# Experts' slot tables by a product with one-hot slots on chip, and three smaller moves, in a hybrid encoder block

## The chip, the core and the metric

One core of a Trainium2 chip runs the whole program. The metric is the device time of one execution in microseconds (us). Before the change three runs took 1166.63, 1168.26 and 1171.79 us; their median, 1168.26, is the time that the change is held against. The engines are TensorE (PE, with its weight loads as PEld), VectorE (DVE), ScalarE (ACT), GpSimd (POOL) and SyncE (SP), which here issues most of the DMAs.

## The reference, cut to what matters

`x` is 1024 tokens of 1024 float32. A mixing part (gated linear attention and indexer-selected attention, merged by gates) gives `mixed`. Then come the output projection, a norm and a two-level mixture of 32 experts, of which each token takes two:

```python
x = x + mixed @ w_out
h = rms_norm(x, g_ffn)
g_logits = h @ w_rg + b_rg                     # 4 groups
g_sel, g_w = argmax(g_logits), softmax(g_logits)[g_sel]
top_v, top_i = top_k((h @ w_re + b_re)[group g_sel], 2)   # of 8 experts in the group
top_w = softmax(top_v) * g_w
for e in range(32):
    hid = silu(h @ w_gate[e]) * (h @ w_up[e])  # D_EXPERT = 128
    y += combine[:, e] * (hid @ w_down[e])
x = x + y
```

## The kernel before, in words

Everything up to the output projection is untouched. Tokens lie in eight tiles of 128. The order of work on each engine is set by a planner that goes by the order of the program and its own cost estimates; a few orders are written out by hand with `add_manual_dep` (SCHED: order of issue only; SYNC: a real wait).

**Projection stage** (lines 821 to 922). `project(i, hf)` multiplies tile i by half `hf` of `w_out` (512 columns): 24 products, three for each of eight blocks of rows, since both factors are split into a high and a low float32r part. `norm_half` adds `x` (line 848, VectorE, into `x1`), transposes the half tile (851), copies it out (852, ScalarE), multiplies it by the 36 router columns (854) and sums squares (857). `norm_route` does the second half, writes `x1` to `out` (866, GpSimd's queue), takes the root by a chain of small VectorE operations (870 to 876), forms the logits (877) and, in `rows`, multiplies the whole row by the root and the gain (881, VectorE) and writes it to `h2d` in DRAM (886, GpSimd's queue).

**Routing.** `Moe.route(i0, i1)` does tiles 0-1, 2-3, 4-5 in pairs between the projections, then tile 6 and tile 7 each by itself. First-of-maximum (1002 to 1006) is five VectorE operations, used for the group and for each of two experts. The choice of a tile is `cn` (128 tokens x 32 experts, 0 or 1). Its rank in the expert comes from two small products per tile (1028 with a triangle of ones, 1031 with the counts so far). From the rank, the slot number is formed (1048 to 1054), and an indirect DMA per tile and pick (1056, GpSimd) scatters the pair (token, weight) to a table `tab` in DRAM with a row for each slot and expert; at the start it was filled with out-of-range tokens. An expert has 96 slots (R = 96) in the main pass.

**Between routing and experts**, `finish_routing` loads the first 96 rows of the table to SBUF (1067, ScalarE's queue), and counts the blocks of 96 beyond the first that each expert needs (1080 to 1095). That list goes to DRAM and back as one row (1097, 1099).

**Experts** (`Moe.run`). For each of 32 experts: gather 96 rows of `h2d` by the table's tokens (1142, GpSimd, indirect), transpose them (1151) and split them (1153, 1154), split the weights (1127 on ScalarE, 1128 on VectorE), multiply by gate and up (1135), form the hidden row (1162 to 1164), transpose it (1169), multiply by down (1177), scale by the token's weight (1180, 1182), and scatter with addition to `out` (1185, GpSimd, indirect). Gathers run five experts ahead in four buffers; `AC` is a ring of four buffers for results. Weights (1.5 MB an expert) are loaded on SP's queue (967, 970, 971) to eight buffers, the first eight experts' during the projection stage. From the ninth on, the gate half's load waits until the gather three experts ahead of the buffer's last user has landed (`late`), and the rest stands behind it or is put ahead by the planner. The first four gathers are issued together; buffers 3 and 4 are cleared before that (1111).

**End.** Each engine reads the number of further blocks from the list (1225), and a loop (1226) runs over them; in these runs its body is not entered. Line 1266 is the code that closes the program.

The `[P, ...]` scratch `V(kb, n)` is a place in one large SBUF tile `G`, which is why so many rows below are named G.

Of the kernel before, what the change touches and what calls it, by code (L numbers as in the profile page):

```python
# [61 lines left out]
def _constants():  # L62
# [20 lines left out]
    oh = np.zeros((P, 512 + 2 * NE * NB), np.float32)  # L83
    oh[:, 384:512] = np.eye(P)[::-1]
    oh[:, 512:512 + NE * NB] = np.repeat(np.arange(NE), NB)[None, :]
    oh[:, 512 + NE * NB:] = np.tile(np.arange(NB) + 1, NE)[None, :]
# [8 lines left out]
def block_kernel(ctx, tc, x, g_mix, w_in, w_alpha2, b_alpha, g_gla, w_br_gla, g_q, g_k, rel_bias, w_br_att,  # L95
# [702 lines left out]
    x1t = [p5.tile([P, 1024], F32, name=f"x1{j}")[:, :] for j in range(3)]  # L798
    h2t = [V(53, 1024), p5.tile([P, 1024], F32, name="h2b")[:, :]]
# [29 lines left out]
    def project(i, hf):  # L829
        if hf == 0:  # L830
            pws[i] = bankA(f"pw{i}")
        mm3(pws[i][:, hf, :], KT, lambda k: mh[i % 2][:, k, :], lambda k: ml[i % 2][:, k, :],
            lambda k: woh[hf][:, k, :], lambda k: wol[hf][:, k, :])
# [6 lines left out]
    def norm_half(i, hf):  # L840

        x1, h2 = x1t[i % 3], h2t[i % 2]
        hT = hTt.rearrange("p (k t) -> p k t", k=KT)
        if hf == 0:
            parts[i] = bankC(f"plg{i}"), ring("ss2", 2, 2)
        plg, ss = parts[i]
        xh = x1[:, 512 * hf:512 * hf + 512]
        nc.vector.scalar_tensor_tensor(xh, pws[i][:, hf, :], 0.5, xh, op0=ALU.mult, op1=ALU.add)
        pt = bankB(f"ph{i}{hf}").rearrange("p (b t) -> p b t", b=4)
        for k in range(4):  # L850
            nc.tensor.transpose(pt[:, k, :], xh[:, k * P:(k + 1) * P], ident)
        nc.scalar.activation(hT[:, 4 * hf:4 * hf + 4, :], pt, AF.Copy)
        for k in range(4 * hf, 4 * hf + 4):
            q = nc.tensor.matmul(plg[:, :36], hT[:, k, :], wr[:, k, :], start=(k == 0), stop=(k == KT - 1))
            if i == NT - 1 and k == 4:
                after(q, moe.rank)
        nc.scalar.activation(h2[:, 512 * hf:512 * hf + 512], xh, AF.Square, accum_out=ss[:, hf:hf + 1])
        if hf == 0:
            nc.vector.tensor_scalar(ss[:, 0:1], ss[:, 0:1], 1.0 / D, EPS, op0=ALU.mult, op1=ALU.add)

    def norm_route(i):
        ts_ = slice(i * P, (i + 1) * P)
        x1, h2 = x1t[i % 3], h2t[i % 2]
        norm_half(i, 1)
        plg, ss = parts.pop(i)
        nc.gpsimd.dma_start(out[ts_, :], x1)
        dump(f"x1_{i}", x1)
        rs = ring("rs", 1, 2)
        v, t, r = (ring(f"{k}_1", 1, 2) for k in ("nv", "nt", "nr"))
        nc.vector.scalar_tensor_tensor(v, ss[:, 1:2], 1.0 / D, ss[:, 0:1], op0=ALU.mult, op1=ALU.add)  # L870
        nc.vector.tensor_scalar(r.bitcast(I32), v.bitcast(I32), 1, None, op0=ALU.logical_shift_right)
        nc.vector.tensor_scalar(r.bitcast(I32), r.bitcast(I32), -1.0, float(MAGIC), op0=ALU.mult, op1=ALU.add)
        nc.vector.tensor_scalar(v, v, -0.5, None, op0=ALU.mult)
        for k in range(3):
            nc.vector.scalar_tensor_tensor(t, r, v, r, op0=ALU.mult, op1=ALU.mult)
# [3 lines left out]
        def rows(late=None):  # L879

            q = nc.vector.scalar_tensor_tensor(*(t.rearrange(m, k=KT) for t, m in (
                (h2, "t (k p) -> t k p"), (x1, "t (p k) -> t k p"))), rs, gffn.rearrange("t (p k) -> t k p", k=KT),
                op0=ALU.mult, op1=ALU.mult)
            if late:
                after(q, late)
            nc.gpsimd.dma_start(h2d[ts_, :], h2)
        return rows
# [9 lines left out]
    for i in range(NT):  # L897
# [6 lines left out]
        if i:  # L904
            if i == NT - 1:
                project(i - 1, 1)
            norm_route(i - 1)()
        norm_half(i, 0)
# [6 lines left out]
        else:  # L915
            project(i, 1)
        if i and i % 2 == 0:
            moe.route(i - 2, i)
    moe.route(6, 7)
    rows = norm_route(7)  # L920
    rows(moe.route(7, 8))
# [6 lines left out]
    moe.finish_routing(dump)  # L928
    if stop == "disp":
        return  # L930
    moe.run(vp2, stop)


class Moe:


    def __init__(self, nc, tc, V, C, bankA, bankB, bankC, drp, h2d, out, lg, tab, onehot, w_gate, w_up, w_down, ident, raws):
# [8 lines left out]
        self.feb = V(57, 2 * NE * NB)  # L946
        nc.sync.dma_start(self.feb, onehot[:, 512:])
# [12 lines left out]
    def load(self, j, wg=None, wu=None, wd=None, late=None):  # L960
# [9 lines left out]
        nc.sync.dma_start(raw[0][:, 1024:2048], wu.rearrange("(p k) c -> p (k c)", p=P))  # L970
# [3 lines left out]
    def route(self, i0, i1, early=None):  # L974
# [25 lines left out]
        def first_max(dst, src, tie, w, m):  # L1000

            nc.vector.tensor_reduce(m, src, axis=AX.X, op=ALU.max)
            nc.vector.tensor_tensor(dst, src, bc(m[:, :, None], [P, n, w]), op=ALU.is_equal)
# [6 lines left out]
        tmp, eg = big(n, 4, 8), big(n, 8)  # L1010
        nc.vector.tensor_mul(tmp, el, bc(ohg[:, :, :, None], [P, n, 4, 8]))
        nc.vector.tensor_reduce(eg, tmp.rearrange("p i g e -> p i e g"), axis=AX.X, op=ALU.add)
# [4 lines left out]
        s1, s2 = big(n, 4, 8), big(n, 4, 8)  # L1017
        cn = tmp
        for s, oh in ((s1, oh1), (s2, oh2)):
            nc.vector.tensor_mul(s, bc(ohg[:, :, :, None], [P, n, 4, 8]), bc(oh[:, :, None, :], [P, n, 4, 8]))  # L1020
        nc.vector.tensor_add(cn, s1, s2)
        cnf = cn.rearrange("p i g e -> p i (g e)")
        for i in range(n):
            nc.vector.tensor_add(self.cum[:, i0 + i + 1, :], self.cum[:, i0 + i, :], cnf[:, i, :])
        pp = self.bankB(f"prank{i0}")
        for i in range(n):
            s = slice(i * NE, (i + 1) * NE)
            q = nc.tensor.matmul(pp[:, s], C("lt"), cnf[:, i, :], start=True, stop=False)
            if early:
                self.tc.add_manual_dep(q.ins, early.ins.name, SCHED, reason="order of issue")  # L1030
            self.rank = nc.tensor.matmul(pp[:, s], C("ones"), self.cum[:, i0 + i, :], start=False, stop=True)
# [6 lines left out]
        nc.vector.tensor_reduce(gs, ex, axis=AX.X, op=ALU.add)  # L1038
        nc.vector.scalar_tensor_tensor(gs, dd, 1.0, gs, op0=ALU.add, op1=ALU.mult)
        nc.vector.tensor_scalar(gs, gs, 2.0, None, op0=ALU.mult)  # L1040
        nc.vector.reciprocal(w12[:, 0, :], gs)
        nc.vector.tensor_mul(w12[:, 1, :], w12[:, 0, :], dd)
        pos, rowf = big(n, NE), big(2, n)
        row = big(2, n).bitcast(I32)
        val = big(2, n, 2)
        nc.vector.tensor_copy(val[:, :, :, 0].bitcast(I32), bc(C("tok")[:, None, i0:i1], [P, 2, n]))
        nc.vector.tensor_copy(val[:, :, :, 1], w12)
        nc.vector.scalar_tensor_tensor(pos, pp[:, :n * NE].rearrange("p (i e) -> p i e", i=n), float(NE),
                                       bc(C("iota_e")[:, None, :], [P, n, NE]), op0=ALU.mult, op1=ALU.add)
        for k, s in enumerate((s1, s2)):  # L1050
            s = s.rearrange("p i g e -> p i (g e)")
            nc.vector.tensor_mul(s, pos, s)
            nc.vector.tensor_reduce(rowf[:, k, :], s, axis=AX.X, op=ALU.add)
            last = nc.vector.tensor_copy(row[:, k, :], rowf[:, k, :])
            for i in range(n):
                s = nc.gpsimd.indirect_dma_start(
                    out=self.tab, out_offset=bass.IndirectOffsetOnAxis(ap=row[:, k, i:i + 1], axis=0),
                    in_=val[:, k, i, :].bitcast(I32), in_offset=None, bounds_check=SLOTS * NE - 1, oob_is_err=False)
# [3 lines left out]
        return last  # L1062

    def finish_routing(self, dump):
        nc, C, V, tab = self.nc, self.C, self.V, self.tab
        tabs = self.tabs = self.keep(NE * 2).rearrange("p (e w) -> p e w", e=NE)
        nc.scalar.dma_start(tabs[:R].rearrange("p e w -> p (e w)").bitcast(I32),
                          tab[0:R * NE, :].rearrange("(s e) w -> s (e w)", e=NE))
        dump("tabs", tabs[:R])

        o = [12 * 256]

        def big(m):
            o[0] += m
            assert o[0] <= 18.5 * 256
            return V(o[0] / 256 - m / 256, m)
# [18 lines left out]
        self.routed = nc.vector.tensor_copy(lsti[:, 3:4], tot)  # L1095
        lstd = self.drp.tile([P, 4], I32, name="lstd")
        nc.scalar.dma_start(lstd, lsti)
        self.lrow = V(26, 512, I32)
        nc.scalar.dma_start(self.lrow[0:1, :], lstd.rearrange("p w -> (p w)")[None, :])
# [14 lines left out]
    def run(self, vp, stop):  # L1114
        nc, tc, V, ident = self.nc, self.tc, self.V, self.ident
        self.begin(vp, 1)
        NR, XG = len(self.raws), self.XG
        AC = [V(o, 1024) for o in (68, 72, 53, 12)][:4]
        HD = [V(57 + 1.5 * j, 384) for j in range(2)]
# [77 lines left out]
        idx = lambda j: self.tabs[:R, self.order[j], 0:1].bitcast(I32)  # L1197
        wgt = lambda j: self.tabs[:R, self.order[j], 1:2]
# [9 lines left out]
        for j in range(NE):  # L1208
# [16 lines left out]
        ntot = nc.values_load(self.lrow[0:1, 3:4], min_val=0, max_val=24)  # L1225
# [45 lines left out]
```

## Time and profile before

| | |
|---|---|
| median of three runs | 1168.26 us |
| profiled execution | 1172.33 us, span 1170.5 us |
| TensorE busy | 1083.0 us (93% of the span) |
| VectorE busy | 886.5 us (76%) |
| ScalarE, GpSimd busy | 506.7 us, 306.4 us |
| mean granted TensorE clock | 0.968 |
| DMA | 140.16 MB, mean 120 GB/s |

The profile is one execution. Times in it are from the span's start. In a row of the timeline the bracket gives the idle time of the engine before the instruction and who ended it; in the chain, each row is one link of the work that ended last. Busy engines off that chain cost nothing.

### The profile page before, as it was taken

To read this page: it belongs to the slowest core of one execution; us is meant where nothing else is said; L and a number is where in the kernel's file an instruction comes from. 1 tells how busy PE (TensorE), PEld (TensorE's weight loads), DVE (VectorE), ACT (ScalarE), POOL (GpSimd) and SP (SyncE) were. 2 spreads that over 40 slices of the span, in tenths; PEclk is the share of its full clock that TensorE was granted. 3 is DMA by queue.
4 is the path that set the end of the run, shared out by engine and by line. 5 is a ranking of instruction groups with operands and counts; after the bars stand their busy time and mean duration, and the time that the engine had idled before them with its cause. 6 is when DMAs were issued, how large, how long until landed. Compare 5 with 4: busy or idle time off the path is not lost.

```text
span 1170.5 us, 18890 instructions
## 1 busy us (share of the span) xinstructions
PE 1083.0 (93%) x7068; PEld 921.2 (79%) x7068; DVE 886.5 (76%) x1747; ACT 506.7 (43%) x1126; POOL 306.4 (26%) x259
## 2 busy tenths in 40 slices
PE   6999998999999999999999999998999659989883
PEld 5998897988788889999867888887778547767662
DVE  5689999999999999994388795552656667866662
ACT  5565626231211125554578764111222226655551
POOL 0100025231131131121043200161022356654422
PEclk9999999999999999999999999998999869998987
DMA  7111111034223231110001006575442669999982
GB/s 255 37 37 37 39 37 39 25 103 145 72 96 121 72 106 58 38 37 18 1 19 38 29 28 227 168 255 168 152 136 91 216 193 292 274 253 287 295 257 40
DMA packets 73104, 140.16 MB, mean 120 GB/s; under 512 B 12282, under 2 KB 47283, under 8 KB 73012
## 3 DMA queue, kind: packets, MB, share of 16 engines
q1 hardware_dynamic: 62482, 112.67, 29.3%
q0 software_dynamic: 10272, 26.25, 8.5%
q8 instruction: 56, 0.92, 0.3%
q14 instruction: 36, 0.29, 0.1%
q10 hardware_dynamic: 258, 0.03, 0.0%
HBM read 115.54 MB, written 31.76 MB: 126 GB/s over the span
## 4 chain that ended last, share of the span: by engine, by line
PE 61%; DVE 17%; DMA 12%; issue 4%; ACT 3%; POOL 0%; SPq 0%; POOLq 0%; DVEq 0%; ACTq 0%
PE pg L236 15%; PE pqkv L236 8%; PE py L236 7%; PE pw L236 5%; DVE G L717 4%; PE pgu L1135 4%; DMA raw<-in_w_gate_dram 4%; PE pv L236 4%; DVE G L716 3%; PE pav L641 3%; DVE G L387 3%; PE pPT L628 3%; PE pidx L236 3%; DMA rawx<-in_w_up_dram 2%; DMA raw<-in_w_down_dram 2%
## 5 line engine op out<-in xcount | busy, mean ns | idle before, releaser
L716 DVE MAX8 G<-G 128x8 f32<-128x384 f32 (+5 forms) x192 | 171.0, 893 | 4.6
L717 DVE MATCH_REPLACE8 G<-G 128x384 f32<-128x384 f32 (+5 forms) x192 | 168.0, 875 | 0.0
L236 PE MATMUL pg<-Qa,Q 128*128 128x512 f32 x512 | 159.8, 392 | 0.0
L228 POOL TENSOR_TENSOR Q<-G,Q 128x2048 fp32r<-128x2048 f32 x13 | 60.8, 4676 | 214.9 <-ACT Q L227 214.9
L236 PEld LDWEIGHTS pg<-Qa,Q 128*128 128x128 f32 x512 | 96.0, 188 | 21.0 <-issue 0.9
L236 PE MATMUL pg<-Qb,Q 128*128 128x512 f32 x256 | 99.6, 389 | 0.0
L236 PE MATMUL pv<-Q,Qa 128*128 128x256 f32 x512 | 94.8, 285 | 0.0
L236 PE MATMUL pqkv<-Q,Qa 128*128 128x256 f32 x512 | 92.2, 283 | 0.0
L236 PEld LDWEIGHTS pv<-Q,Qa 128*128 128x128 f32 x512 | 80.1, 191 | 2.1 <-issue 1.5
L236 PEld LDWEIGHTS pqkv<-Q,Qa 128*128 128x128 f32 x512 | 79.9, 192 | 0.1
L1185 POOL DMA_INDIRECT out_dram<-G x32 | 55.8, 1745 | 65.5 <-ACT G L1180 21.7
L236 PE MATMUL pv<-Q,Qb 128*128 128x256 f32 x256 | 72.5, 283 | 0.0
L236 PE MATMUL pqkv<-Q,Qb 128*128 128x256 f32 x256 | 72.5, 283 | 0.0
L227 ACT ACTIVATE Q<-G 128x2048 fp32r<-128x2048 f32 x20 | 38.2, 1911 | 78.4 <-PE pg L236 77.0
L1135 PE MATMUL pgu<-Qb,xt0h 128*96 128x256 f32 x256 | 54.4, 311 | 6.9 <-ACT xt0h L1153 6.9
L596 POOL TENSOR_TENSOR sm<-Tb,G 128x256 f32<-128x256 f32 x48 | 35.3, 741 | 96.0 <-DVE G L614 62.6
L1142 POOL DMA_INDIRECT xg<-h2d,G x32 | 47.7, 1491 | 46.1 <-DVE xt0l L1154 20.6
L236 PEld LDWEIGHTS pg<-Qb,Q 128*128 128x128 f32 x256 | 48.1, 188 | 10.2 <-issue 0.5
L1128 DVE TENSOR_TENSOR Qb<-G,Qb 128x1024 fp32r<-128x1024 f32 x32 | 38.6, 1217 | 21.2 <-ACT Qb L1127 21.0
L1135 PEld LDWEIGHTS pgu<-Qb,xt0h 128*96 128x96 f32 x256 | 40.6, 182 | 17.5 <-ACT xt0h L1153 17.4
L619 ACT ACTIVATE sm<-sm,G 128x128 f32<-128x128 f32 (+7 forms) x64 | 49.3, 771 | 7.2 <-DVE G L614 6.6
L1135 PE MATMUL pgu<-Qb,xt1h 128*96 128x256 f32 x256 | 51.8, 303 | 0.0
(292 smaller groups left out, 2870.7 us busy)
## 6 DMA issues: line engine op xcount, KB each, us to landing
G<-in_w_in_dram SPq DMA_DIRECT2D x20, 1024.0 KB, 5.2
gd<-G SPq DMA_DIRECT2D x16, 512.0 KB, 2.6
G<-gd SPq DMA_DIRECT2D x16, 512.0 KB, 4.5
G<-in_w_down_dram SPq DMA_DIRECT2D x16, 512.0 KB, 16.7
G<-in_w_gate_dram SPq DMA_DIRECT2D x16, 512.0 KB, 13.5
G<-in_w_up_dram SPq DMA_DIRECT2D x16, 512.0 KB, 20.8
raw<-in_w_gate_dram SPq DMA_DIRECT2D x12, 512.0 KB, 10.3
raw<-in_w_up_dram SPq DMA_DIRECT2D x12, 512.0 KB, 18.4
```

The source lines that it names most:

```text
L227: nc.scalar.activation(hi, r3, AF.Copy)
L228: (eng or nc.vector).tensor_sub(lo, r3, f(hi))
L236: nc.tensor.matmul(o, a, b, start=(i == 0), stop=(i == len(seq) - 1))
L387: nc.vector.scalar_tensor_tensor(scv, rl, wisc[:, i, h:h + 1], scv, op0=ALU.mult, op1=ALU.add)
L596: nc.gpsimd.tensor_tensor(band, Tb[:, h, :], sc[i][:, n1:], op=ALU.add)
L619: nc.scalar.activation(sm[:, :W], sm[:, :W], AF.Exp, scale=-1.0, bias=nm[:, 1:2], accum_out=rs8s[i][:, h:h + 1])
L716: nc.vector.max(out=m8, in_=sc[i])
L717: nc.vector.match_replace(out=sc[i], in_to_replace=m8, in_values=sc[i], imm_value=SENT)
L1128: q = nc.vector.tensor_sub(lo[:, n], r, hi[:, n].bitcast(F32))
L1135: nc.tensor.matmul(o, a, b, start=(i == 0), stop=(i == len(seq) - 1))
L1142: gathered[j] = nc.gpsimd.indirect_dma_start(out=XG[j % 4][:R], out_offset=None, in_=self.h2d, in_offset=bass.IndirectOffsetOnAxis(ap=idx, ...
L1185: return nc.gpsimd.indirect_dma_start(out=self.out, out_offset=bass.IndirectOffsetOnAxis(ap=idx, axis=0), in_=AC[j % 4][:R], in_offset=Non ...
```

## The change

- **One-hot slots.** `route` becomes `choose`, `place` and `enter`. `choose` makes the picks as before (one operation less in a first-of-maximum of a single tile), and masks `s` (expert of pick k) and `ve` (the same times token - 1024, and times weight). `place` reduces each pick's rank to one number per token (`tensor_tensor_reduce`), compares it with 0..95 to a one-hot `S` (128 tokens x 96 slots), and multiplies `S` transposed by `ve` on TensorE: the result, added to `acc` (which starts as 1024 and 0), is the table on chip, slots x experts. For the last two tiles the token half is multiplied and written first (`routed`), the weight half after. `enter` still scatters to the table in DRAM, for the further blocks alone; for the last two tiles it does so after the first four gathers.
- **Rows.** The row times gain is formed by GpSimd in parts (`norm_part`), the factor of the root is applied by ScalarE (`norm_rows`), and the writes to `h2d` and `out` go out on ScalarE's queue, `h2d` first.
- **Two lots.** The last tile's second half is projected and normalised in two lots of 256 columns, and tile 6's rank products are ordered after tile 7's logits.
- **Counting** moves behind expert 26's split, its two DMAs to SP's queue, and the read of the number of blocks behind expert 29. A GpSimd `drain` is added after the last gather.
- **Weights.** The up half waits for the gather too, as the gate half did.

```diff
-    def norm_half(i, hf):
+    def norm_part(i, c0, n=512):
...
-        nc.scalar.activation(h2[:, 512 * hf:512 * hf + 512], xh, AF.Square, accum_out=ss[:, hf:hf + 1])
+        sq = ring("ssq", 1, 4)
+        nc.scalar.activation(sqj[:, :n], xh, AF.Square, accum_out=sq)
...
+        nc.gpsimd.tensor_mul(h2.rearrange("t (k p) -> t k p", k=KT)[:, :, c0 // KT:(c0 + n) // KT],
+                             *(t[:, c0:c0 + n].rearrange("t (p k) -> t k p", k=KT) for t in (x1, gffn)))
+        return q
...
+        nc.scalar.activation(h2, h2, AF.Copy, scale=rs)
+        nc.scalar.dma_start(h2d[ts_, :], h2)
+        nc.scalar.dma_start(out[ts_, :], x1)
...
-    moe.route(6, 7)
-    rows = norm_route(7)
-    rows(moe.route(7, 8))
+    for c0 in (512, 768):
+        project(NT - 1, c0, 256)
+    for c0 in (512, 768):
+        q = norm_part(NT - 1, c0, 256)
+    ch = [moe.choose(NT - 2, NT - 1, q)]
+    norm_rows(NT - 1)
+    ch.append(moe.choose(NT - 1, NT))
+    moe.place(ch, True)
...
-        nc.sync.dma_start(raw[0][:, 1024:2048], wu.rearrange("(p k) c -> p (k c)", p=P))
+        q = nc.sync.dma_start(raw[0][:, 1024:2048], wu.rearrange("(p k) c -> p (k c)", p=P))
+        if late:
+            self.tc.add_manual_dep(q.ins, late.ins.name, SYNC, reason="the tokens' rows come first")
...
+    def place(self, chs, last=False):
+        nc, V = self.nc, self.V
+        o = [16 * 256]
+        mms = []
+        for c in chs:
+            for k in range(2):
+                for i in range(c["n"]):
+                    rk = c["rk"][:, k, i:i + 1]
+                    q = nc.vector.tensor_tensor_reduce(out=c["jk"], in0=c["s"][k][:, i, :], in1=c["pp"][:, i * NE:(i + 1) * NE],
+                                                       scale=1.0, scalar=0.0, op0=ALU.mult, op1=ALU.max, accum_out=rk)
+                    if c is not chs[-1]:
+                        self.tc.add_manual_dep(q.ins, chs[-1]["chosen"].ins.name, SCHED, reason="the last tile's choice first")
+                    S = V(o[0] / 256, R)
+                    o[0] += R
+                    nc.vector.tensor_scalar(S, self.slot, rk, None, op0=ALU.is_equal)
+                    mms.append((S, c["ve"][:, k, i]))
+        pt = chs[-1]["pp"][:R, 256:256 + 2 * NE]
+        def product(c0, c1):
+            for m, (S, ve) in enumerate(mms):
+                nc.tensor.matmul(pt[:, c0 * NE:c1 * NE], S, ve[:, c0:c1].rearrange("p w e -> p (w e)"),
+                                 start=(m == 0), stop=(m == len(mms) - 1))
+        if last:
+            product(0, 1)
+            self.routed = nc.vector.tensor_tensor(self.tabs[:R, 0, :].bitcast(I32), pt[:, :NE], self.acc[:R, :NE], op=ALU.add)
+        for c in chs:
+            c["weigh"]()
+        product(1 if last else 0, 2)
+        if last:
+            nc.vector.tensor_add(self.tabs[:R, 1, :], pt[:, NE:], self.acc[:R, NE:])
+            return
+        nc.vector.tensor_add(self.acc[:R], pt, self.acc[:R])
+        for c in chs:
+            self.enter(c)
...
-        for j in range(4):
-            first = gather_x(j, idx(j)) if j < 2 else gather_x(j, idx(j)) and first
+        for j in range(2):
+            gather_x(j, idx(j))
+        self.begin(vp, 1)
+        NR = len(self.raws)
+        for j in range(2, 4):
+            gather_x(j, idx(j))
+        for c in chs:
+            self.enter(c)
...
+            if j == NE - 6:
+                self.count_blocks(dump)
+                tc.add_manual_dep(nc.gpsimd.drain().ins, gathered[NE - 1].ins.name, SCHED, reason="after the last gather")
+            if j == NE - 3:
+                ntot = nc.values_load(self.lrow[0:1, 3:4], min_val=0, max_val=24)
```

## Rows read from the trace of the kernel before

**Rows 1.** Stages: span; PE, PEld, DVE, ACT, POOL busy us; clock; DMA share; GB/s
```profile
935.00:941.00 6.00, 0.00 (x0) 0.00 (x0) 5.86 (x10) 0.00 (x0) 5.64 (x5) 0.50 0.14 53
...
941.00:954.00 13.00, 4.00 (x22) 3.73 (x23) 5.38 (x10) 1.62 (x2) 7.61 (x7) 0.50 0.64 186
...
1046.00:1127.00 81.00, 65.10 (x392) 49.07 (x390) 47.09 (x64) 39.94 (x66) 32.23 (x21) 0.91 0.95 285
...
1127.00:1154.00 27.00, 25.32 (x145) 19.24 (x145) 16.34 (x24) 12.06 (x23) 8.28 (x5) 0.90 0.52 141
```

**Rows 2.** Chain of waits across the hole: start us, us, what
```profile
923.22 0.68 DVE x L848
...
938.03 2.22 DMA tab<-G
...
940.27 1.99 DMA G<-tab
...
943.12 8.25 DMA xg<-h2d,G x2
```

**Rows 3.** Timeline of the routing: start us, us, engine, line, operation
```profile
925.17 0.38 PE L1028 MATMUL prank<-G 128*128 128x32 f32 x2 [2.00 <-DVE G L871]
...
928.40 0.26 DVE L877 SCALAR_TENSOR_TENSOR G<-plg,G 128x36 f32<-128x36 f32 x1 [0.46 <-PE plg L854]
...
932.77 0.19 DVE L1024 TENSOR_TENSOR G<-G 128x32 f32<-128x32 f32 x1
...
933.96 0.19 DVE L1048 SCALAR_TENSOR_TENSOR G<-prank,G 128x32 f32<-128x32 f32 x1 [0.92 <-PE prank L1031]
...
949.74 1.51 PE L1151 MATMUL pxg<-G,xg 96*128 96x96 f32 x8 [15.39 <-DMA xg<-h2d,G]
```

**Rows 4.** Timeline of GpSimd before the experts
```profile
939.67 1.85 POOL L1111 MEMSET xg<- 128x1024 f32 x2
...
943.12 2.55 POOL L1142 DMA_INDIRECT xg<-h2d,G  x1 [1.59 <-DMA G<-tab]
...
948.51 0.96 POOL L1142 DMA_INDIRECT xg<-h2d,G  x1 [0.30 <-issue]
```

**Rows 5.** Timeline of SP's DMA queue: weight loads
```profile
941.76 3.39 SPq L970 DMA_DIRECT2D G<-in_w_up_dram  x2
...
953.82 2.21 SPq L967 DMA_DIRECT2D G<-in_w_gate_dram  x2
```

**Rows 6.** Groups by form, then by line: instructions nearest to those added or removed
```profile
L614 DVE CUSTOM_DVE_ANT_0 sm<-pL,Tb,G 128x128 f32<-128x128 f32 x8 | 2.8, 350 | 4.2 <-PE pPT L628 3.4 <-PE pL L605 0.5
...
L614 DVE DVE_READ_ACCUMULATOR2_ANT G<- 128x1 f32 x64 | 5.3, 82 | 0.0
...
L783 POOL TENSOR_TENSOR G<-G x16: 1282/1288/3219, 757.1 to 796.8; 128x512 f32<-128x512 f32 x16
...
L881 DVE SCALAR_TENSOR_TENSOR h2b<-x,G 128x1024 f32<-128x1024 f32 x4 | 8.9, 2236 | 0.1
```

**Rows 7.** Chain of waits: the expert stage
```profile
994.02 23.26 DMA raw<-in_w_down_dram
...
1144.38 1.72 PE py L1177 x4
```

**Rows 8.** Closing code's drains; DMA issues: count, KB, us to landing
```profile
L1266 POOLq DRAIN  x3: 46/104/8076, 1161.6 to 1170.2; - x3
...
xg<-h2d,G POOLq DMA_INDIRECT x32, 9.1
...
tab<-G POOLq DMA_INDIRECT x16, 4.2
...
h2d<-h2b POOLq DMA_DIRECT2D x4, 512.0 KB, 4.0
```

**Rows 9.** The block list: its DMA, and its read by ScalarE
```profile
lstd<-G ACTq DMA_DIRECT2D x1, 2.0 KB, 4.3
...
L1225 ACTq TENSOR_LOAD <-G x1: 1379/1379/1379, 1154.4 to 1154.4; - x1
```

More of the change, by code (lines that the diff above doesn't have):

```diff
@@ L798, in block_kernel @@
     x1t = [p5.tile([P, 1024], F32, name=f"x1{j}")[:, :] for j in range(3)]
+    sqj = p5.tile([P, 512], F32, name="sqj")
     h2t = [V(53, 1024), p5.tile([P, 1024], F32, name="h2b")[:, :]]
@@ L838, in block_kernel @@
     parts = {}
-    def norm_half(i, hf):
+    def norm_part(i, c0, n=512):
         x1, h2 = x1t[i % 3], h2t[i % 2]
         hT = hTt.rearrange("p (k t) -> p k t", k=KT)
-        if hf == 0:
-            parts[i] = bankC(f"plg{i}"), ring("ss2", 2, 2)
+        if c0 == 0:
+            parts[i] = bankC(f"plg{i}"), [ring("ssp", 1, 8), None]
         plg, ss = parts[i]
[L847 to L853, printed above, removed]
-            q = nc.tensor.matmul(plg[:, :36], hT[:, k, :], wr[:, k, :], start=(k == 0), stop=(k == KT - 1))
-            if i == NT - 1 and k == 4:
-                after(q, moe.rank)
-        nc.scalar.activation(h2[:, 512 * hf:512 * hf + 512], xh, AF.Square, accum_out=ss[:, hf:hf + 1])
-        if hf == 0:
-            nc.vector.tensor_scalar(ss[:, 0:1], ss[:, 0:1], 1.0 / D, EPS, op0=ALU.mult, op1=ALU.add)
@@ L861, in norm_route @@
-    def norm_route(i):
+        xh = x1[:, c0:c0 + n]
+        k0, k1 = c0 // P, (c0 + n) // P
+        nc.vector.scalar_tensor_tensor(xh, pws[i][:, c0 // 512, c0 % 512:c0 % 512 + n], 0.5, xh, op0=ALU.mult, op1=ALU.add)
+        pt = bankB(f"ph{i}{c0}").rearrange("p (b t) -> p b t", b=4)
+        for k in range(k0, k1):
+            nc.tensor.transpose(pt[:, k - k0, :], x1[:, k * P:(k + 1) * P], ident)
+        nc.scalar.activation(hT[:, k0:k1, :], pt[:, :k1 - k0, :], AF.Copy)
+        for k in range(k0, k1):
+            q = nc.tensor.matmul(plg[:, :36], hT[:, k, :], wr[:, k, :], start=(k == 0), stop=(k == KT - 1))
@@ L862, in norm_route, with norm_rows @@
+        return q
+    def norm_rows(i):
         ts_ = slice(i * P, (i + 1) * P)
         x1, h2 = x1t[i % 3], h2t[i % 2]
[L864 to L867, printed above, removed]
+        plg, (v, _) = parts.pop(i)
         rs = ring("rs", 1, 2)
-        v, t, r = (ring(f"{k}_1", 1, 2) for k in ("nv", "nt", "nr"))
-        nc.vector.scalar_tensor_tensor(v, ss[:, 1:2], 1.0 / D, ss[:, 0:1], op0=ALU.mult, op1=ALU.add)
+        t, r, hv = (ring(f"{k}_1", 1, 2) for k in ("nt", "nr", "nv"))
@@ L914, in block_kernel @@
             moe.begin(vp, 2)
-        else:
-            project(i, 1)
+        elif i < NT - 1:
+            project(i, 512)
         if i and i % 2 == 0:
-            moe.route(i - 2, i)
-    moe.route(6, 7)
-    rows = norm_route(7)
-    rows(moe.route(7, 8))
+            moe.place([moe.choose(i - 2, i)])
+    for c0 in (512, 768):
[6 more added lines that the diff above has]
+    moe.place(ch, True)
     dump("lg", lg)
@@ L1047, in route @@
[L1047 to L1055, printed above, removed]
+        val, ek, rk = big(2, n, 2), big(2, n), big(2, n)
@@ new lines, in rows @@
+        def rows():
+            nc.vector.tensor_copy(val[:, :, :, 0].bitcast(I32), bc(C("tok")[:, None, i0:i1], [P, 2, n]))
+            nc.vector.tensor_copy(val[:, :, :, 1], w12)
+            for k in range(2):
+                for i in range(n):
+                    nc.vector.tensor_tensor_reduce(out=jk, in0=ss[k][:, i, :], in1=C("iota_e"), scale=1.0, scalar=0.0,
+                                                   op0=ALU.mult, op1=ALU.max, accum_out=ek[:, k, i:i + 1])
+        return dict(n=n, pp=pp, s=ss, ve=ve, jk=jk, ek=ek, rk=rk, val=val, chosen=chosen, weigh=weigh, rows=rows,
+                    row=big(2, n))
@@ L1056, in route, with enter @@
+    def enter(self, c):
+        nc = self.nc
+        row = c["row"].bitcast(I32)
+        c["rows"]()
+        nc.vector.scalar_tensor_tensor(row, c["rk"], float(NE), c["ek"], op0=ALU.mult, op1=ALU.add)
+        for k in range(2):
+            for i in range(c["n"]):
                 s = nc.gpsimd.indirect_dma_start(
                     out=self.tab, out_offset=bass.IndirectOffsetOnAxis(ap=row[:, k, i:i + 1], axis=0),
-                    in_=val[:, k, i, :].bitcast(I32), in_offset=None, bounds_check=SLOTS * NE - 1, oob_is_err=False)
+                    in_=c["val"][:, k, i, :].bitcast(I32), in_offset=None, bounds_check=SLOTS * NE - 1, oob_is_err=False)
@@ L1061, in route, with count_blocks @@
                 self.scs.append(s)
[L1062 to L1071, printed above, removed]
+    def count_blocks(self, dump):
+        nc, C, V = self.nc, self.C, self.V
+        o = [int(23.3 * 256)]
         def big(m):
             o[0] += m
-            assert o[0] <= 18.5 * 256
-            return V(o[0] / 256 - m / 256, m)
+            assert o[0] <= 28 * 256
+            return V((o[0] - m) / 256, m)
         feb = self.feb
```

124 lines of the change are left out of this document (67 added, 57 removed).

## The prediction

> **What bounds the kernel now.** I read the stage table first, then the chain of waits, then the queues. The stage table [rows 1] shows a hole: from 935 to 941 us TensorE did nothing, from 941 to 954 it was busy 4.00 of 13 us, at a granted clock of 0.50. From 1046 to 1127 the DMA engines are the busy ones (share 0.95, 285 GB/s) while TensorE has 65.1 of 81 us. In the last stage, 1127 to 1154, TensorE is the bound again (25.3 of 27 us) and the DMA share is down to 0.52.
>
> The chain says what the hole is made of [rows 2]: the last projection tile leaves PSUM at 923.22, the last table scatter is in flight from 938.03 (2.22 us), the table comes back from DRAM in 1.99 us from 940.27, and the first two gathers of token rows fly from 943.12 for 8.25 us. In between is the choice of experts, a row of small VectorE instructions: the last logits at 928.40, the last of the choice at 932.77, the ranks read at 933.96 [rows 3]. Then the first expert's transpose starts at 949.74, after 15.39 us of waiting for its rows.
>
> What comes behind matters as much. The ninth expert's weights go out when the fourth gather has landed, at 953.82 [rows 5], and from 994.02 the chain runs through DMA, piece after piece (the first of them 23.26 us) [rows 7]. So an earlier start is worth what it gives to the weight stream, not to TensorE. Third, a look at the end: of GpSimd's three drains in the closing code the longest takes 8.076 us, the others 0.046 and 0.104 [rows 8], and nothing else runs meanwhile.
>
> **The change part by part.** All times in the profiled execution, 1172.33 us (span 1170.5), which is 4.07 us over the median of 1168.26; I subtract the sum from the median.
>
> *Last projection in two lots.* 24 products of 512 columns become 48 of 256, the same columns: 0. The last lot's tail is half as long: evacuation was 0.68 us [rows 2], now about 0.4. Also, today the ranks of tile 6 stand ahead of tile 7's transposes on TensorE and make it wait 2.00 us from 923.17 [rows 3]; the new order puts them behind the logits. From 923.22 to the logits at 928.40 it is 5.2 us; I take off 1.9 (bounds 0 and 2.6: the 2.00 plus a shorter copy and square).
>
> *Choice.* From 928.40 to the end of line 1024 (932.77 + 0.19) stand 22 instructions in turn, 0.207 us each. With one tile, each of three maxima loses one, and the sum over two picks loses one: 4 x 0.207 = 0.8 us. Choice done at 932.96 - 1.9 - 0.8 = 930.3.
>
> *One-hot product in place of the DRAM table.* On VectorE follow: the running count, two masks and two masked token numbers (5 x 0.19 = 0.95, by line 1048), then for two tiles and two picks a reduction over 32 experts and a comparison with 96 slots. The trace has neither. The reduction is 0.35 us at 128 columns plus 0.08 for the accumulator [rows 6], so at most 0.43, and no less than 0.19; I take 0.33. The comparison lies between 0.19 and 0.35; I take 0.25. Four pairs: 2.3 us (1.5 to 3.1). The ranks' product (0.38 per two now [rows 3]) is hidden by that. Then the last of four products and the addition that writes the indices, 0.3 + 0.2, and the hand-over to GpSimd, 0.2. First gather at 930.3 + 0.95 + 2.3 + 0.7 = 934.3, against 943.12: 8.8 us (6 to 10).
>
> What is late next: tile 7's rows in DRAM. They need ScalarE's scaling (at most the 2.24 us that VectorE takes [rows 6]) and a write of 4.0 us [rows 8] behind a root that is known by 926.5: 932.7 at the latest. It holds by 1.5 us. Behind the scaling on ScalarE stand only the write of `out` and copies that need the gathers.
>
> *Gathers and the weight stream.* The first gather took 2.55 us to issue, the fourth went out 5.39 us after it and landed 5.31 us later [rows 4, 5]. The two buffer clears took 1.85 us ahead of the first; if they now stand between the second and third, as program order has them, that costs 1.9 and a quicker first issue gives back 1.5. So the weights are released at 934.3 + 5.4 + 0.4 + 5.3 = 945.4, 8.4 us earlier. But the second halves of two experts, which now go out from 941.76 on, within 3.39 us [rows 5], must wait as well: 1.05 MB at 285 GB/s is 3.7 us of DMA work that is no longer done in the hole. The DMA share of 0.64 before 954 leaves room to make up part; I take 1.5 as lost (0 to 3.7). Net 6.9 us, rounded to -6.5 for the four table scatters (about 1.3 us each) that now stand on GpSimd ahead of the fifth gather; what the DMA engines have to move behind it does not change, so I let the whole stage shift by that.
>
> *Projection stage.* Three pairs of tiles get four products each of 64 columns: 12 x 0.19 = 2.3 us on a TensorE that is full there, if none hides. VectorE loses eight multiplications of about 2.2 us [rows 6] that were no bound, GpSimd gains sixteen of 1.29 us (as line 783, if its stride costs no more) with room. DMA starts move from GpSimd to ScalarE's queue, 16 of them. Sum +1 (between -2, if stalls behind the VectorE passes go, and +4, if TensorE also waits for the one-hots).
>
> Here a rule speaks against the change. The rows show that a GpSimd issue takes 2.55 us where VectorE works on two SBUF inputs and 0.96 just after [rows 4]. The Trainium skill (SBUF — State Buffer, "SBUF: two separate sides") says that the shared port pair is an exclusive lock for a whole instruction, between VectorE operations with two SBUF inputs and GpSimd operations that read SBUF. The first row agrees. By the rule the last tile's GpSimd multiplication would hold up the chain of the root by its own length, half of line 783's 1.29, and the sum would be 0.65 us worse.
>
> *Block counting and loads at expert 26 and 29.* VectorE was busy 5.86 of 6 us from 935 to 941, most of it counting and one large row product; it was hidden by the table's trip, so taking it away there gives 0. In its new place it stands beside the wait for the last weights, yet behind it come the products of expert 28 in a stage that TensorE bounds. Then each engine reads the list in the middle of that stage, ScalarE in 1.38 us [rows 9]. +1 (0 to 4).
>
> *One more drain.* If the long drain's time goes with the DMAs issued on GpSimd since the last one, it is spread over 80 indirect ones (16 table scatters, 32 gathers [rows 8], a scatter for each of 32 experts) or more: 0.1 us each. Behind the new drain remain six scatters: 0.6 us. That is -7.5 at the end. The new drain itself, 7 to 8 us, falls into GpSimd's pauses between scatters and is hidden; without that cover a scatter goes out a few us late, and four accumulator buffers stand behind it. If the cost is fixed, or comes from something else in the closing code, the gain is 0, so the bounds are -7.6 and 0 (+0.1 for a second short drain). I take -7.5: the other two drains, with nothing issued before them, cost next to nothing.
>
> Sum: -6.5 + 1 + 1 - 7.5 = -12. 1168.26 - 12 = 1156.3, rounded to 1156.
>
> **Rivals.**
> *The drain's cost is fixed.* Both drains take 8 us, the first hidden. For it: one long drain cannot show a slope. Then -6.5 + 2 = -4.5: 1164.
>
> *The weight stream swallows the early start.* DMA is the bound from 994, and 3.7 us of loads leave the hole; if the clears and table scatters keep the loads back another 3 us, the stage gains 8.4 - 3.7 - 3 = 1.7 us. With the drain: -1.7 + 2 - 7.5 = -7.2: 1161. Against: the share of 0.64 in the hole.
>
> *The list comes too late (slower).* All five engines now read the block list after expert 29's down projection, which ended at 1146.10 (1144.38 + 1.72 [rows 7]). The list needs two trips to DRAM behind the count, which stands behind expert 28's split, some three experts earlier: with five experts in the last stage's 25.3 us, 15 us earlier, and 3 us of counting (an estimate), it ends at 1134. One trip landed in 4.3 us in the hole [rows 9]; gathers in the busy stage have a median of 9.1 [rows 8]. Two trips at 4.3 plus issue are 10 us and arrive in time. If both wait behind queued weights for as long as the 23.26 us piece [rows 7], the list lands at 1180.5, 34 us after TensorE wants it, and the balance is -12 + 34 = +22: 1190. It decides above 12 us of stall, a landing after 1158. Against: the DMA share is 0.52 after 1127.
>
> **How the numbers follow.** Forecast 0.56, spread about 4 us: 0.55 of it faster by more than 0.5% (5.8 us, about what a measurement of this kernel tells from no change; the line is 1162.4). Fixed drain 0.22: 0.07 faster, the rest no change. Stream swallows 0.12: 0.07 faster, the rest no change. Late list 0.07, all slower. 0.03 is left for several small losses: 0.02 no change, 0.01 slower. Faster 0.55 + 0.07 + 0.07 = 0.69, no change 0.01 + 0.15 + 0.05 + 0.02 = 0.23, slower 0.08. Range: the terms' bounds around 1156 go to 1149, and up to 1167 the fixed drain is held.
>
> **What would show it.** Right: the first expert's transpose near 940 instead of 949.74; no load of the table ahead of the first gather; weights released near 945; a second long GpSimd drain near the last gather and a final one under 1 us. Wrong: a final drain still near 8 us; the DMA stage from 994 ending where it did though its start is earlier; TensorE waiting on lines of the projection stage for one-hots; engines idle together before expert 30, at the read of the list.

## The result, and the profile after

The changed kernel took 1177.99 us (median of 5 runs, 1175.63 to 1179.88) where the kernel before took 1169.26 in the same session: ratio 1.0082, 95% interval 1.0066 to 1.0099. It is slower by 8.7 us; 1156 was predicted. Its profiled execution took 1178.37 us, with a span of 1176.5.

First the stage table of the kernel after (columns as in [rows 1]): the projection stage as a whole, and then the stages of [rows 1].

```profile
780.00:936.40 156.40, 139.97 (x706) 112.56 (x706) 81.89 (x317) 37.18 (x69) 59.79 (x38) 0.96 0.39 137
...
941.00:954.00 13.00, 4.01 (x20) 3.63 (x20) 11.06 (x65) 3.34 (x5) 4.31 (x3) 0.50 0.56 175
...
1046.00:1127.00 81.00, 61.58 (x386) 46.58 (x385) 47.59 (x65) 40.62 (x67) 34.41 (x22) 0.96 0.92 283
...
1127.00:1154.00 27.00, 23.49 (x146) 18.40 (x145) 19.74 (x34) 14.22 (x24) 8.43 (x5) 0.94 0.88 269
```

TensorE has 139.97 busy us in 156.4: the projection stage ends at 936, not at 924, and at 941 to 954 the routing still runs. The last stage, 1127 to 1154, now has a DMA share of 0.88 where [rows 1] had 0.52: the weight stream is late there too. The chain of waits shows one place of the projection stage, its end and the hole (start us, us, what):

```profile
867.71 0.70 DVE x L854
868.55 3.37 POOL h2b L871
871.91 1.81 issue
873.73 1.16 ACT h2b L889
874.91 0.33 ACTq L890
875.29 0.60 ACT hT L858
...
935.70 0.75 DVE x L854 x2
936.45 1.08 DVE G L1037
...
941.80 0.27 DVE G L888
...
949.59 0.58 issue
950.39 0.48 POOL xg L1208
```

GpSimd's product and ScalarE's row scaling stand in the chain, ahead of the copy of the transposed tile (`hT`) for which TensorE waits; neither was in the chain before. The last half tile leaves PSUM from 935.70 on, both lots together in 0.75 us (923.22 in [rows 2]), and the first gather goes out at 950.39 (943.12 in [rows 4]). The ninth expert's weights follow on SP's queue at 963.68 (953.82 in [rows 5]), now with the up half behind the gate half:

```profile
963.68 0.33 SPq L980 DMA_DIRECT2D G<-in_w_gate_dram  x1
964.12 0.56 SPq L983 DMA_DIRECT2D G<-in_w_up_dram  x1
```

At the end the drains (ns min/median/max) answer to [rows 8]:

```profile
L1296 POOLq DRAIN  x1: 14652/14652/14652, 1128.5 to 1128.5; - x1
...
L1342 POOLq DRAIN  x3: 46/98/623, 1175.1 to 1176.2; - x3
```

The long closing drain fell from 8.076 to 0.623 us, and the new one takes 14.65 us in the middle, to 1143.19; the next scatter goes out at 1144.11. The last scatter is issued at 1169.18, after expert 31's down projection, so no scatter that ends the program waits for the new drain.

The balance between the two profiled executions, by the weights' release: +9.9 at 963.68; the last expert's gate product is +13.9 (1145.53 to 1159.48), so about 4 more came in the weight stream; -7.45 at the drain: +6.4, against +6.0 in the spans.

One number of [rows 2] needs a word. In the kernel before TensorE ran below full clock from 800 to 820 in the profiled execution; the later kernel `e10`, which issues the same work there, did not. In the kernel before it had been idle for 2.30 us, to 807.84, and then ran at half clock (0.50, the lower of its two levels, 1.2 and 2.4 GHz, from 808.2 to 814.9); in `e10` the same gap was 1.23 us. First before, then `e10`:

```profile
800.00:820.00 20.00, 17.70 (x69) 14.28 (x68) 3.01 (x6) 2.99 (x6) 0.60 (x1) 0.83 0.46 181
```

```profile
800.00:820.00 20.00, 18.77 (x96) 15.05 (x94) 6.91 (x18) 4.82 (x10) 0.60 (x1) 1.00 0.60 234
```

`e10` begins its last evacuation at 918.74, 4.5 us earlier than before; 1.4 us of that is an earlier start of the stage (805.68 against 807.10), the rest the gap and the clock. From the start of the first evacuation to that of the last half tile it is 116.1 us before, 113.1 in `e10` and 129.8 after, so the stage grew by 13.7 to 16.7 us, more than the 12.5 between 923.22 and 935.70. That is why medians carry the verdicts below and single profiles only the mechanism.

### The profile page after: what moved, and what is told of

It is laid out like the page before. It is cut to its first block, busy times and chain, and to the rows that moved or that the text cites. A ratio compares the mean times of both kernels' runs of the same rounds, so it can differ in the third digit from the quotient of the medians.

```text
span 1176.5 us, 19128 instructions
## 1 busy us (share of the span) xinstructions
PE 1090.2 (93%) x7132; PEld 926.0 (79%) x7132; DVE 895.4 (76%) x1815; ACT 516.1 (44%) x1137; POOL 331.4 (28%) x262
## 4 chain that ended last, share of the span: by engine, by line
PE 61%; DVE 17%; DMA 13%; issue 4%; ACT 4%; POOL 1%; SPq 0%; ACTq 0%; POOLq 0%; DVEq 0%
PE pg L238 15%; PE pqkv L238 8%; PE py L238 7%; DMA raw<-in_w_gate_dram 6%; PE pw L238 4%; DVE G L719 4%; PE pv L238 3%; PE pav L643 3%; DVE G L718 3%; PE pgu L1201 3%; PE pPT L630 3%; PE pidx L238 3%; DMA raw<-in_w_down_dram 2%; DVE G L389 2%; DMA rawx<-in_w_up_dram 2%
## 5 line engine op out<-in xcount | busy, mean ns | idle before, releaser
L1251 POOL DMA_INDIRECT out_dram<-G x32 | 53.3, 1667 | 69.1 <-ACT G L1246 26.3
```

The lines of the kernel that those rows point to most:

```text
L1251: return nc.gpsimd.indirect_dma_start(out=self.out, out_offset=bass.IndirectOffsetOnAxis(ap=idx, axis=0), in_=AC[j % 4][:R], in_offset=Non ...
```

## The experiments

Theory: GpSimd's product of row and gain, and the row scaling behind it on ScalarE, lengthen the projection stage. Rivals: the one-hot products do; or the loss is in the weight stream.

**What is the drain worth, and what do the rows cost?** `e1` is before plus the drain:

```diff
+            if j == NE - 6:
+                tc.add_manual_dep(nc.gpsimd.drain().ins, gathered[NE - 1].ins.name, SCHED, reason="after the last gather")
```

> The kernel before with one more GpSimd drain behind the last gather, nothing else. Theory (a drain's length goes with the DMAs issued on GpSimd since the last one): the closing long drain falls from 8.08 to about 0.6 us, the new one takes 12 to 15 us beside the work of TensorE and delays nothing: 7.4 us under before, about 1162. Rival (the new drain holds up the scatters that follow, or the last gathers' experts): the gain at the end is given back, within 2 us of before.

1164.19 us, ratio 0.9949 [0.9933, 0.9965]: 5.6 us faster. The drains are 14.97 and 0.623 us. An early drain takes over what the closing one would take, and the rival falls; the interval (4.1 to 7.8 us) does not tell 5.6 from 7.4. That the length goes with the number of DMAs is not shown: 90 of GpSimd's queue stood ahead of the 14.97 us, 98 ahead of the 8.08 us in the kernel before.

`e2` is after with the rows of seven tiles formed as before; `e3` is before with the rows of after:

```diff
+        if i < NT - 1:
+            nc.gpsimd.dma_start(out[ts_, :], x1)
+            nc.vector.scalar_tensor_tensor(... rs, gffn ..., op0=ALU.mult, op1=ALU.mult)
+            nc.gpsimd.dma_start(h2d[ts_, :], h2)
+        else:
...
```

> The kernel after, but the rows of tiles 0 to 6 are formed by VectorE in one operation again and written from GpSimd's queue (the last tile stays with GpSimd and ScalarE). Theory (GpSimd's strided product and ScalarE's in-order row scaling are what lengthens the projection stage): the last projection product leaves PSUM about 9 us earlier (near 927 instead of 935.7), and the whole is 8 to 11 us faster than after, about 1167 to 1170. Rival (the one-hot products and their waits on TensorE lengthen it): at most 3 us of the stage come back, about 1175.

> The kernel before with the rows of all tiles formed by GpSimd and ScalarE and written from ScalarE's queue, nothing else. Theory (rows lengthen the projection stage): the last projection product leaves PSUM 8 to 11 us later (931 to 934 instead of 923.2), and the whole is 6 to 11 us slower than before, about 1175 to 1180. Rival (one-hot products lengthen it): within 2 us of before.

`e2`: 1161.55, 0.9929 [0.9914, 0.9944], 16.4 us under after, more than the theory's 11; last evacuation from 923.28 on. `e3`: 1184.25, 1.0131 [1.0112, 1.0151], 14.5 us over before; last evacuation at 932.75, or 126.7 us after its first. Both runs say the same from two sides: the rows cost about 15 us, the one-hot products little. By the profile of `e3`, 10.6 us of its loss stand in the projection stage (126.7 against 116.1) and 4.4 behind it, between last evacuation and first gather (24.3 against 19.9).

**Which part of the rows?** Three kernels, each after with one piece moved: `e6` forms the product on VectorE (tiles 0 to 6), `e7` scales on GpSimd, `e8` keeps GpSimd's product but in the columns' own order. `e8` leaves out the reordering of the columns that the experts need; it stands here for its time alone.

```diff
-        nc.gpsimd.tensor_mul(h2.rearrange(...)[...], ...)
+        mul = nc.vector.tensor_mul if i < NT - 1 else nc.gpsimd.tensor_mul     # e6
+        mul(h2.rearrange(...)[...], ...)
...
+            nc.gpsimd.tensor_scalar(h2, h2, rs, None, op0=ALU.mult)            # e7, for i < NT - 1
...
+        nc.gpsimd.tensor_mul(h2[:, c0:c0 + n], x1[:, c0:c0 + n], gffn[:, c0:c0 + n])   # e8
```

> The kernel after, but the product of row and gain of tiles 0 to 6 is formed by VectorE, in the same two parts; ScalarE still scales the rows and issues the writes. Theory A (GpSimd's long product and its hold on VectorE cost the stage): 9 to 13 us faster than after, about 1166, last projection product out of PSUM near 925. Theory B (ScalarE's scaling, in order ahead of its copies of the transposed tile, costs the stage): less than 4 us faster than after, about 1175.

> The kernel after, but the scaling by the root of tiles 0 to 6 is done by GpSimd, behind its product, and the writes go out on GpSimd's queue; ScalarE has neither. Theory A (GpSimd's product and its hold on VectorE): no better than after, 1177 to 1182. Theory B (ScalarE's order): 9 to 13 us faster than after, about 1166. If each has a share: between.

> The kernel after, but GpSimd's product keeps the order of a row's columns; the reordering of the columns is left out. If the stride is what makes the product long, a 128x512 product takes about 1.29 us instead of 2.32. Theory A then gives back half of the stage's loss, 5 to 8 us, about 1171; theory B gives at most 3 us, about 1176, since ScalarE's scaling still waits for the root.

`e6`: 1158.78, 0.9909 [0.9894, 0.9923], 19 us under after: theory A, and beyond it. `e7`: 1173.19, 1.0031 [1.0019, 1.0044], 5 us under after. It does not price ScalarE's order by itself, since each scaling now takes GpSimd 2.86 us; against a large share of ScalarE stands `e6`, which keeps the scaling there and has a stage of 111.3 us, shorter than before's. `e8`: 1166.47, 0.9974 [0.9962, 0.9986], 11.5 us under after: most of the loss is the product's length, and its length is the stride. The groups by form (us in all, mean ns | idle before them), VectorE's split `ml` and the product, first after:

```profile
L827 DVE TENSOR_TENSOR ml<-G,mh 128x1024 fp32r<-128x1024 f32 x8 | 19.2, 2406 | 0.6 <-ACT mh L826 0.4
L871 POOL TENSOR_TENSOR G<-x,G 128x512 f32<-128x512 f32 x8 | 18.6, 2320 | 37.7 <-DVE x L854 37.7
```

then `e8`, with the columns in order:

```profile
L827 DVE TENSOR_TENSOR ml<-G,mh 128x1024 fp32r<-128x1024 f32 x8 | 15.1, 1890 | 0.6 <-ACT mh L826 0.4
...
L871 POOL TENSOR_TENSOR G<-x,G 128x512 f32<-128x512 f32 x8 | 10.3, 1284 | 41.4 <-DVE x L854 41.4
```

and `e6`:

```profile
L827 DVE TENSOR_TENSOR ml<-G,mh 128x1024 fp32r<-128x1024 f32 x8 | 10.9, 1361 | 0.0
L872 DVE TENSOR_TENSOR G<-x,G 128x512 f32<-128x512 f32 x8 | 9.6, 1203 | 0.2
```

Strided, GpSimd needs 2.32 us for what VectorE does in 1.20; in order it needs 1.28. And a VectorE operation in which nothing was changed, `ml`, goes from 2.41 to 1.89 to 1.36 us as GpSimd's product gets shorter and goes away.

Not all that `e6` gave back is the product. In after, VectorE stood from 853.9 to 859.7 behind the landing of a scatter to the table in DRAM, with the logits behind that wait in its order; TensorE's next router product waited 2.86 us, and within this gap its clock fell to half (0.50 from 858.9 to 865.6). These rows of VectorE and TensorE are of after:

```profile
859.72 0.17 DVE L1074 CAST G<-G 128x4 int32<-128x4 f32 x1 [5.82 <-DMA tab<-G]
859.83 0.26 DVE L888 SCALAR_TENSOR_TENSOR G<-plg,G 128x36 f32<-128x36 f32 x1
```

```profile
860.24 1.90 PE L860 MATMUL plg<-G,hT 128*128 128x36 f32 x8 [2.86 <-DVE G L866]
```

and these of VectorE are of `e6`, where the planner put the logits ahead of the wait, and TensorE has no such gap:

```profile
850.24 0.25 DVE L889 SCALAR_TENSOR_TENSOR G<-plg,G 128x36 f32<-128x36 f32 x1 [0.32 <-PE plg L860]
856.59 0.17 DVE L1075 CAST G<-G 128x4 int32<-128x4 f32 x1 [6.10 <-DMA tab<-G]
```

The stretch from 860 to 870 (columns of [rows 1]), first after, then `e6`:

```profile
860.00:870.00 10.00, 9.76 (x35) 8.17 (x36) 2.34 (x5) 1.78 (x3) 1.46 (x1) 0.72 0.07 27
```

```profile
860.00:870.00 10.00, 9.45 (x53) 7.71 (x52) 8.33 (x49) 3.15 (x7) 0.00 (x0) 1.00 0.51 160
```

The kernel before has the gap too (2.86 us to 858.25, clock 0.86 from 860 to 870), and so have `e3` (3.37) and `e8` (2.79); `e2`, `e6` and `e7` have not. With half of the 6.7 us at half clock added, some 6 us of what `e2` and `e6` gave back can be this order of VectorE's work (an estimate from these rows; no run moves the order alone), and it may be all of `e7`'s 5. `e3` and `e8`, which keep the gap, price the rows and the stride without it.

**The waiting up half.** `e4` frees it in after, `e5` in `e2`, `e9` in `e6`; `e10` puts the wait alone into before.

```diff
-        q = nc.sync.dma_start(raw[0][:, 1024:2048], wu...)
-        if late:
-            self.tc.add_manual_dep(q.ins, late.ins.name, SYNC, ...)
+        nc.sync.dma_start(raw[0][:, 1024:2048], wu...)
```

> The kernel after, but the up half of an expert's weights waits for no gather, as in the kernel before. Theory (the weight stream bounds the experts, so the two up halves, 1.05 MB or 3.7 us of DMA work, are fully lost when they leave the hole): 3.7 us faster than after, about 1174, with the shift of the last expert's gate product against before down from 13.9 to about 10 us. Rival (the wait costs nothing, or up loads in the hole slow the gathers): same as after, or up to 2 us slower.

> The rows of tiles 0 to 6 on VectorE as in the experiment before that put them back, and the up half of the weights free of the gather as well. Theory (the two losses are independent, the weight stream bounds from expert 16): 3.5 to 4.5 us faster than rows back alone (1161.6), about 1157.5, so some 12 us under before. Rival (with the projection stage short again the up halves no longer bound): within 1.5 us of 1161.6.

> Product of tiles 0 to 6 on VectorE, and the up half of the weights free of the gather. Freeing it gave 3.4 us in the kernel after and nothing with the rows back on VectorE. Theory (the stream bounds only while the experts start late): within 1.5 us of 1158.8. Rival (the loads of the hole are lost whenever they wait): 3 to 4 us faster, about 1155.

> The kernel before, with the up half of the weights waiting for the gather as the gate half does, nothing else. By the term of the prediction as the traces corrected it (3.7 us of DMA work leave the hole, nothing is given back): 3 to 4 us slower than before, about 1173. If the gathers land earlier for it and give it back: within 1.5 us of before.

`e4`: 1174.60, 1.0041 [1.0029, 1.0054], 3.4 us under after. `e5`: 1162.63, 0.9939 [0.9924, 0.9955], no gain over `e2`'s 1161.55, so the theory of two independent losses fell there. `e9`: 1156.72, 0.9889 [0.9867, 0.9911], 2.1 under `e6`, intervals overlapping. `e10`: 1169.52, 1.0007 [0.9992, 1.0022]: the wait alone cost nothing.

`e13` (after) and `e15` (`e12`, below) free the gate half as well, `e14` is `e12` with the up half free:

```diff
-        if late:
-            self.tc.add_manual_dep(q.ins, late.ins.name, SYNC, ...)     # of the gate half, e13 and e15
```

> The kernel after with neither the gate half nor the up half of the weights waiting for a gather: up to 2.1 MB, 7.4 us of DMA work at 285 GB/s, can go into the hole. Theory (the weight stream bounds, what leaves the hole is lost): some 7 us faster than after, about 1171. Rival (what the loads gain, the gathers of the first experts lose beside them): 1173 to 1178, no better than with the up half alone free (1174.6).

> All products on VectorE and the up half free. By the two gains measured so far for a free up half in a kernel like the changed one (3.4 and 2.1 us): 1153.5 to 1155 against 1156.8 with the wait. If the price is nil, as the wait alone in the kernel before and the rows put back say: 1156 to 1158.

> All products on VectorE, gate and up halves free. Theory (stream bound): 3 us under the kernel with the up half alone free, about 1151 to 1152. Rival (the gathers lose it): the same or slower, 1155 to 1159, with the first expert's gate product later than with the wait.

`e13`: 1176.48, 1.0058 [1.0040, 1.0076]: no better than `e4`. Its first expert's gate product starts at 963.75, 3.2 us later than in `e4`, and the last expert's is as much behind. Its second gather landed 9.4 us after its issue began, that of `e4` 6.7. `e14`: 1153.49, 0.9864 [0.9844, 0.9885]. `e15`: 1155.40, 0.9869 [0.9848, 0.9890], no better than `e14`. So loads in the hole take time from the first gathers: the up half of two experts was worth 2.1 to 3.4 us in three of five pairs of kernels (only `e4` has an interval clear of its partner's), and the gate half nothing. Why the wait cost nothing in `e10` and in `e2` stays open.

**Drain and hole once more.** `e11` is `e6` without the drain; `e12` forms the last tile's product on VectorE too (`nc.vector.tensor_mul` throughout).

> Product of tiles 0 to 6 on VectorE, without the new drain. Theory (the drain is worth its 7.4 us wherever the end lies): about 1165.5, with a closing drain of 8 us. Rival (part of it goes to the scatters that the long drain in the middle holds up, as 5.6 us measured for the drain alone may say): 1162.5 to 1164.

> Product on VectorE for all tiles, the last one too. In the hole two VectorE operations of tile 6 took 1.1 us each beside GpSimd's last two products, and the root of tile 7 started 1.6 us after its last square. Theory (GpSimd's hold delays the choice of experts): the two fall to 0.2 us, VectorE gains two products of 0.6 us, and the first gather comes 0.5 to 1.5 us earlier: 1157.5 to 1158.5. Rival (VectorE's own products in the chain cost more than the hold): 1159 to 1160.5.

`e11`: 1165.20, 0.9959 [0.9945, 0.9973]: the drain is worth 6.4 us there, with a closing drain of 6.77. `e12`: 1156.81, 0.9893 [0.9872, 0.9915], 2 us under `e6` with overlapping intervals; the first gather comes 14.0 us after the last evacuation instead of 14.6.

`e14` is faster than both kernels, by 16 us than before. Its projection stage:

```profile
780.00:917.00 137.00, 133.08 (x708) 109.42 (x706) 79.47 (x329) 35.95 (x69) 23.92 (x22) 1.00 0.46 157
```

About as many products as after, in 137 us at full clock, and TensorE waits for no one-hot there. They still take its time: `e5` has 50 more TensorE instructions in this stage than `e10` and 2.3 us more busy time (110.28 against 108.00), about what the prediction allowed for them.

## Why the prediction was wrong

**Projection stage, +1 (bounds -2 to +4): the step that failed.** The rows alone cost 14.5 us (`e3`), 10.6 of them in this stage, and gave back 16.4 (`e2`). Between the two profiles the stage grew by 13.7 us (116.1 to 129.8), not by 1. Two sub-steps were wrong. The price: "1.29 us, if its stride costs no more" was the row of line 783, whose operands are contiguous; the strided product took 2.32. The cover: "with room" asked whether GpSimd has time, not who waits meanwhile. The timelines of VectorE, GpSimd and ScalarE in the kernel after show it at one place:

```profile
868.50 1.22 DVE L827 TENSOR_TENSOR ml<-G,mh 128x1024 fp32r<-128x1024 f32 x1
869.64 2.28 DVE L868 SCALAR_TENSOR_TENSOR G<-G 128x1 f32<-128x1 f32 x1
```

```profile
868.54 3.36 POOL L871 TENSOR_TENSOR h2b<-x,G 128x512 f32<-128x512 f32 x1 [9.21 <-DVE x L854]
```

```profile
873.73 1.15 ACT L889 ACTIVATE h2b<-h2b,G 128x1024 f32<-128x1024 f32 x1 [4.51 <-issue]
874.91 0.33 ACTq L890 DMA_DIRECT2D h2d<-h2b  x1
875.29 1.08 ACT L858 ACTIVATE hT<-ph 128x512 f32<-128x512 f32 x2 [0.41 <-PE ph L857]
```

GpSimd's product took 3.36 us instead of 2.32, longer by about the split that VectorE had begun just ahead of it; then an operation on one number per partition, the sum of squares ahead of the root, took 2.28 us instead of 0.15 and ended with the product, at 871.9. The whole root stood behind it, and behind the root ScalarE's scaling and VectorE's evacuation of the next half tile (873.59), on which TensorE's transposes (`ph`) and `hT` wait. Here TensorE itself lost less than 1 us (0.67 for `ph`, 0.24 for `hT`). At another place it lost 2.07:

```profile
814.69 2.32 POOL L871 TENSOR_TENSOR G<-x,G 128x512 f32<-128x512 f32 x1 [5.66 <-DVE x L854]
```

```profile
814.84 3.26 DVE L827 TENSOR_TENSOR ml<-G,mh 128x1024 fp32r<-128x1024 f32 x1 [0.23 <-ACT mh L826]
```

```profile
819.90 0.44 PE L857 MATMUL ph<-G,x 128*128 128x128 f32 x2 [2.07 <-DVE G L887]
```

The split, 1.22 us at 868.50, took 3.26 beside GpSimd's product, and the root and the evacuation stood behind it. Such a gap can cost TensorE twice: behind this one its clock was at half (0.50 from 821.3 to 824.6), while `e6`, idle for 0.34 us there, kept full clock. The stretch from 820 to 825, first after, then `e6`:

```profile
820.00:825.00 5.00, 5.00 (x24) 4.19 (x25) 2.78 (x4) 2.28 (x4) 2.30 (x1) 0.66 0.47 184
```

```profile
820.00:825.00 5.00, 5.00 (x28) 4.13 (x28) 1.16 (x8) 1.69 (x2) 0.00 (x0) 1.00 0.65 256
```

Over the whole stage TensorE was idle for 16.4 us in after and 4.3 in `e6` (span less busy time), and its 706 products took 139.97 busy us against 134.27 for as many, by the clock here and at 860. One of the prediction's own signs of being wrong is in the idle time: TensorE waited 4.2 us for the one-hots, whose comparisons stood on VectorE behind the long splits (one took 3.31 us from 845.80, with the comparisons from 849.04 on), and 1.1 us in `e6`. TensorE's waits by line, first after, then `e6`:

```profile
PE prank L1104 <- DVE G L1092: 2.9, 2, 1.6
...
PE prank L1104 <- issue: 1.3, 1, 1.3
```

```profile
PE prank L1105 <- DVE G L1093: 1.1, 1, 1.1
```

The prediction quoted the Trainium skill's rule on the shared port pair (SBUF — State Buffer, "SBUF: two separate sides") and priced it for the last tile alone, at 0.65 us. The two timelines agree with the rule, their two ends lie 0.02 us apart; it should have been applied to all of the products and to every VectorE operation with two SBUF inputs near them. A second rule was not weighed: the Trainium skill (GPSIMD Engine Reference, "7. Performance pitfalls for Q7 kernels") puts reads with a step of over 8 bytes at 50% more per element. Here the step was 32 bytes and the trace shows 81% more (2.32 against 1.28).

**Choice and one-hot product, first gather 8.8 us earlier.** Between last evacuation and first gather 5.2 us were saved: 19.9 before, 14.7 after. The one-hot part was right: from the end of the choice (945.90) to the written index (949.55) 3.65 us, predicted 3.75. What failed is the 1.9 us taken off ahead of the logits: they come 6.1 us after the last evacuation, and two operations of tile 6 took 1.17 us each beside GpSimd's last products. `e12`, without those, has 4.9, so the hold is some 1.2 of the 2.8 us missed. The two lots gave no shorter tail: both left PSUM together, in 0.75 us. The hand-over took 0.8, not 0.2.

**Release of the weights.** From first gather to release it was 13.3 us, not 11.1: the clears stood between the gathers at 1.85 us as assumed, but the second gather took 3.17 us to issue, beside VectorE's splits. And of the hole's gain little reaches the end: `e5`, which has all of the change but the rows of seven tiles and the up half's wait, is 7.0 us under before, of which the drain is 5.6 to 6.4. In its profile the time from last evacuation to first gather is 4.9 us shorter than in `e10`, but the projection stage is 3.0 longer, 2.3 of it TensorE's own time, and first gather to release 1.1 longer.

**Up halves, 1.5 lost (0 to 3.7).** 3.4 in the kernel after (`e4`): within the bounds, near the wrong end; nothing in `e10` and `e5`.

**Drain, -7.5.** Right in that the closing time goes away, and roughly in size: 7.45 in the profile, 5.6 and 6.4 by medians. The rival of a fixed cost is refuted by the closing 0.623 us. The price of 0.1 us a DMA is not borne out: the new drain took 14.65 us, not 7 to 8, with 74 DMAs ahead of it. What sets its length stays open.

**Counting and list, +1; the rival that it comes too late.** Did not happen: TensorE, VectorE, ScalarE and GpSimd read it from 1166.45 to 1169.12, as the last down projection (1166.23 to 1168.19) ran and after it. No run priced it alone.

The range failed with the projection stage's term: bounds of -2 to +4 for 16 instructions of a form that the trace did not have.

## What to carry to other kernels

Before work goes to an idle GpSimd, take its price from a row with the same strides, and look at what VectorE does at that time: an operation of one number can wait for all of a large product (2.28 us instead of 0.15). Ask of work that moves to an in-order engine what stands behind it there. Loads put into a hole compete with the transfers that end it.

## What the runs showed of the hardware that was not expected

- A GpSimd drain behind over 70 DMAs of its queue took 12.65 to 15.33 us in the middle of the expert stage, and 6.8 to 8.1 us at the end when it was the first; a second one behind seven scatters took 0.62. The length is no fixed price, and about twice as long in the middle as at the end.
- A 128x512 product with a step of 8 elements: 2.32 us on GpSimd, 1.20 on VectorE. A 128x1024 scaling on GpSimd: 2.86 us, on ScalarE 1.15.
- TensorE's granted clock was 0.83 over 20 us in one execution and 1.00 in another at the same work, behind idle times of 2.30 and 1.23 us; with the longer gap it made 3 us of a stage that no edit had touched.
- A wait for a scatter's landing on an in-order engine (5.82 us on VectorE) cost TensorE 2.86 us where the logits stood behind it, and nothing where they stood ahead of it (6.10 us in `e6`).
